# A hybrid encoder layer: the first modulation moved from VectorE to TensorE, filter loads to GpSimd's queue, the last gate computed late

## The chip, the cores and the metric

The kernel runs on one core of a Trainium2 chip. The metric is the device time of one execution in microseconds. Before the change three runs gave 1537.08, 1530.63 and 1531.85 us; the median is 1531.85 us.

The engines are called by their short names: PE is TensorE (matmuls; PEld its weight loads), DVE is VectorE, ACT is ScalarE, POOL is GpSimd and SP is SyncE. SP, ACT and POOL can issue DMAs; a name with q behind it (SPq) is an engine's instruction queue. Every engine executes its instructions in a fixed order.

## The reference

One layer over 1024 positions of width 1024, in float32. A conditioning vector c gives six vectors of 1024 (shift, scale and gate for two sub-layers). The first sub-layer normalises x, scales and shifts it, projects it, runs four mixers on groups of the projection and adds the gated output. The second is a SwiGLU with its own shift, scale and gate.

```python
mod = silu(c) @ mod_w + mod_b              # 6 x 1024
s1, b1, g1, s2, b2, g2 = split(mod, 6)     # shift, scale, gate, twice
u = (rms_norm(x) * (1 + b1) + s1) @ w_in
y = concat(ssd(u), neighbourhood_attention(u), mlstm(u), hyena(u))
x = x + g1 * (y @ w_out)
h = rms_norm(x) * (1 + b2) + s2
x = x + g2 * ((silu(h @ w_gate) * (h @ w_up)) @ w_down)
out = rms_norm(x) * final_g
```

The Hyena mixer convolves with long filters. They come from a small network of sines over the positions (`hyena_mlp`), a last matrix `w3`, a decay in time, a norm over the positions, and a discrete Fourier transform in which 16-point parts are done by additions on DVE and the rest by matmuls with tables. There are two filter orders.

## The kernel before, in words

Precise matmuls are made of three float32r products: a value is split into a high part and a remainder (`split`), and hi\*hi, lo\*hi and hi\*lo are added up in one PSUM bank. The normalised, modulated and transposed input stands in 16 tiles, `hhi[k]` and `hlo[k]` for k = 0 to 7, each 128 x 1024. Projections are groups of 256 columns (`w_group` loads and splits the weights; `gemm_t` makes, for each of two 128-column parts j, two 512-position halves h of 24 matmuls each, L493).

`build` states the order in which work is written down, and a planner of the framework puts each engine's instructions in a fixed order by readiness and that order. So instructions of several stages stand mixed in an engine's queue. The start of the program is written down so:

- `hyena_mlp` (L693 on): two layers of the sine network, each a matmul and seven DVE operations (`sin_layer`, L682 to L687) and one on ACT.
- `start` (L398 on): the first modulation. Its weights, 8 MB, are loaded by SP as 16 tiles of 512 KB into the slots that `hhi` and `hlo` take later (L416). Quarter q holds the shift and scale columns of k = 2q and 2q + 1. For three of the quarters DVE adds up eight weighted tiles into an accumulator of 128 x 512 (L420, L422); for quarter 3 ACT makes the products (L425) and POOL adds them (L427). The sum over partitions comes from transposes on PE and a reduction on DVE (L447, L449).
- Between the second and the third of these rounds the first part of `hyena_filters` (L720 on) is written: for eight blocks of positions a matmul with `w3` (L736), the decay loaded by SP into one of two buffers (L739), and DVE and ACT operations (L741 to L750); the norm is summed on PE (L746).
- Then the eight tiles of x are loaded (L435), squared on ACT (L437), scaled by DVE (L442), and for two halves h and eight k transposed on PE (L460), modulated on ACT (L462) and split (L235 on DVE; the remainder, L239, on POOL for even k and on DVE for odd k).
- The rest of `hyena_filters`: for each order and two sums q the Fourier transform; its nine matmul steps (L763, L765) each need a table that SP loads into one of three buffers (L761).

The second modulation is spread out. `modulation2` (L1485 on) adds up eight 512-column accumulators on DVE from 64 loads of 256 KB (L1494; two load buffers, two accumulators; L1496, L1498), which are stored to DRAM, while the Hyena convolutions and the SSD projections run; `modulation2_sums` (L1504 on) loads them again before the mLSTM and sums over partitions, for the gates g1 and g2 with a matmul by ones, and stores the gates to DRAM (`K.gd`). `attention` loads g1, and `ffn` loads g2 right after its second loop.

`ffn` has two loops over 22 blocks of hidden columns (matmuls at L1603) and a last stage, the down projection (L1742). Its buffers are numbered slots of 4 KB per partition; a tuple of slots is taken in turn. `psr` takes slots 27, 0, 1, 2 in turn, so the last block's `psr` is in slot 0. The last stage's weights are loaded to `wdr` and split to `wdh` and `wdl`:

```python
raw = S.tile([P, 2, H], F32, (17, 9, 10, 11), "wdr")
wh = S.tile([P, 2, H], F32R, (18, 12, 13, 14), "wdh")
wl = S.tile([P, 2, H], F32R, (21, 15, 16, 8), "wdl")
```

## Time and profile before

| | us |
|---|---|
| median of three runs | 1531.85 |
| the profiled execution | 1531.33 |
| its span, first to last instruction | 1529.5 |
| PE busy | 1412.3 (92%) |
| DVE busy | 1043.3 (68%) |
| ACT busy | 527.6 (34%) |
| POOL busy | 91.4 (6%) |

The shares are averages over stages with different limits. Matmuls are pipelined: one that is given as 0.39 us can start 0.23 us behind the one before it, so the distance of two starts, not the length, is what a matmul costs. A float32 matmul (not float32r) appears as two records. A wait is put down to what ended last before the waiting instruction began.

### The profile page before, as it was taken

The numbers are of one execution on the slowest core, as the hardware profiler recorded it, in microseconds if no ns is written. First come the engines' busy times: TensorE is split into PE (matmuls) and PEld (weight loads), VectorE is DVE, ScalarE is ACT, GpSimd is POOL, SyncE is SP. The second block draws the span as 40 slices with busy tenths as digits, with TensorE's granted clock in tenths as the row PEclk, the third lists the DMA queues.
The fourth block names the chain that finished last, engine by engine and source line by source line (L and its number), as shares of the span: only waits on it lengthen the run. The fifth ranks groups of instructions, "written<-read, shape, count | busy, mean of one in ns | idle before, by whom it ended". The sixth has DMA issues, their size and how long they took to land.

```text
span 1529.5 us, 19231 instructions
## 1 busy us (share of the span) xinstructions
PE 1412.3 (92%) x6849; PEld 1141.0 (75%) x6849; DVE 1043.3 (68%) x2004; ACT 527.6 (34%) x958; POOL 91.4 (6%) x143
## 2 busy tenths in 40 slices
PE   2589979998998998989989999999999999999997
PEld 0366768876797777867767777888888888888886
DVE  7998977977847684687865476477777766335327
ACT  2522221232242342333456775322222223224222
POOL 2110000000102231230000000000000000000000
PEclk9789999999998999999999999999999999999999
DMA  6534467577653325476426457554444448643402
GB/s 247 194 104 143 128 197 230 185 225 226 190 185 110 105 87 155 125 265 203 154 87 217 150 170 276 201 180 164 148 144 153 149 164 305 222 149 123 153 1 110
DMA packets 134899, 257.02 MB, mean 168 GB/s; under 512 B 24703, under 2 KB 69663, under 8 KB 134804
## 3 DMA queue, kind: packets, MB, share of 16 engines
q1 hardware_dynamic: 111508, 228.50, 45.4%
q10 hardware_dynamic: 22688, 25.99, 4.8%
q0 software_dynamic: 608, 1.31, 0.3%
q8 instruction: 54, 0.88, 0.2%
q14 instruction: 41, 0.34, 0.1%
HBM read 195.17 MB, written 60.59 MB: 167 GB/s over the span
## 4 chain that ended last, share of the span: by engine, by line
PE 74%; DVE 13%; DMA 5%; issue 2%; ACT 2%; POOL 2%; SPq 0%; DVEq 0%; ACTq 0%; POOLq 0%
PE dps L1742 14%; PE X L1603 12%; PE gps L493 9%; PE Z L1603 8%; PE Y L1603 8%; PE gps L505 4%; PE gps L1554 3%; PE nS L1427 2%; PE ops L1554 1%; DMA mxw<-modw 1%; PE nS L1405 1%; DVE wlo L239 1%; PE kps L763 1%; PE mpa L1339 1%; DVE acc L422 1%
## 5 line engine op out<-in xcount | busy, mean ns | idle before, releaser
L1742 PE MATMUL dps<-wdh,ah 128*128 128x512 f32 x352 | 136.9, 389 | 0.0
L1742 PE MATMUL dps<-wdh,al 128*128 128x512 f32 x352 | 136.9, 389 | 0.0
L1742 PE MATMUL dps<-wdl,ah 128*128 128x512 f32 x352 | 136.9, 389 | 0.0
L493 PE MATMUL gps<-hhi,whi 128*128 128x512 f32 x320 | 130.7, 408 | 3.8 <-ACT nt L529 3.8
L493 PE MATMUL gps<-hlo,whi 128*128 128x512 f32 x320 | 129.6, 405 | 0.0
L493 PE MATMUL gps<-hhi,wlo 128*128 128x512 f32 x320 | 129.0, 403 | 0.0
L1603 PE MATMUL Z<-hp,wgh 128*128 128x512 f32 x352 | 95.4, 402 | 1.9 <-ACT ps L1658 1.6
L239 DVE TENSOR_TENSOR al<-ar,ah 128x1024 fp32r<-128x1024 f32 x44 | 53.4, 1222 | 47.9 <-ACT ah L233 47.9
L505 PE MATMUL gps<-whi,hhi 128*128 128x256 f32 (+1 forms) x256 | 77.5, 303 | 1.5 <-ACT z L529 1.5
L1603 PEld LDWEIGHTS Z<-hp,wgh 128*128 128x128 f32 x352 | 63.7, 188 | 19.8 <-ACT ps L1658 5.3
L505 PE MATMUL gps<-whi,hlo 128*128 128x256 f32 (+1 forms) x256 | 77.2, 302 | 0.0
L505 PE MATMUL gps<-wlo,hhi 128*128 128x256 f32 (+1 forms) x256 | 77.1, 301 | 0.0
L1742 PEld LDWEIGHTS dps<-wdl,ah 128*128 128x128 f32 x352 | 66.1, 188 | 13.8
L1742 PEld LDWEIGHTS dps<-wdh,al 128*128 128x128 f32 x352 | 66.1, 188 | 13.7
L1742 PEld LDWEIGHTS dps<-wdh,ah 128*128 128x128 f32 x352 | 66.1, 188 | 13.6
L493 PEld LDWEIGHTS gps<-hhi,whi 128*128 128x128 f32 x320 | 60.6, 189 | 19.5 <-ACT nt L529 5.0
L493 PEld LDWEIGHTS gps<-hhi,wlo 128*128 128x128 f32 x320 | 60.5, 189 | 13.8 <-issue 1.6
L233 ACT CAST ah<-ar 128x1024 fp32r<-128x1024 f32 x44 | 45.7, 1048 | 72.5 <-PE dps L1742 42.7
L493 PEld LDWEIGHTS gps<-hlo,whi 128*128 128x128 f32 x320 | 60.6, 189 | 12.4 <-issue 0.8
L1603 PE MATMUL X<-A,t4s 128*128 128x512 f32 x264 | 63.4, 389 | 0.0
L239 DVE TENSOR_TENSOR wdl<-wdr,wdh 128x1024 fp32r<-128x1024 f32 x22 | 26.9, 1224 | 53.1 <-ACT wdh L233 53.1
L1498 DVE SCALAR_TENSOR_TENSOR mxacc<-mxw,cond,mxacc 128x512 f32<-128x512 f32 x56 | 42.0, 750 | 29.2 <-DMA mxw<-modw 28.9
(500 smaller groups left out, 3240.5 us busy)
## 6 DMA issues: line engine op xcount, KB each, us to landing
wg<-wg SPq DMA_DIRECT2D x44, 512.0 KB
ar<-ad SPq DMA_DIRECT2D x44, 512.0 KB
mxw<-modw SPq DMA_DIRECT2D x64, 256.0 KB
raw<-w_in SPq DMA_DIRECT2D x28, 512.0 KB
psd<-ps SPq DMA_DIRECT2D x22, 512.0 KB
psr<-psd SPq DMA_DIRECT2D x22, 512.0 KB
wu<-wu SPq DMA_DIRECT2D x22, 512.0 KB
wdr<-wd SPq DMA_DIRECT2D x22, 512.0 KB
```

The lines of the kernel that those rows point to most:

```text
L233: nc.scalar.copy(hi, src)
L239: e.tensor_tensor(lo, src, hi.bitcast(F32), op=ALU.subtract)
L422: V.scalar_tensor_tensor(acc, in0=w, scalar=c, in1=acc, op0=ALU.mult, op1=ALU.add)
L493: nc.tensor.matmul(ps, lhsT=w[:, k, c], rhs=x[k][:, t], start=n == 0, stop=n == len(seq) - 1)
L505: nc.tensor.matmul(ps, lhsT=x[k][:, t], rhs=w[:, k, :N], start=n == 0, stop=n == len(seq) - 1)
L763: nc.tensor.matmul(ps, lhsT=tab[:, la], rhs=y[:, 0], start=True, stop=not cx)
L1339: nc.tensor.matmul(pa[:, 2 * j + dr], lhsT=sds[dr][:, h], rhs=va[:, h], start=True, stop=True)
L1427: nc.tensor.matmul(pb[:, 448:512], lhsT=pT[:w * 40, n], rhs=vw[:w * 40, n, c:c + 64], start=n == 0, stop=n == len(chunks) - 1)
L1498: V.scalar_tensor_tensor(acc, in0=mt, scalar=K.cond[:, k:k + 1], in1=acc, op0=ALU.mult, op1=ALU.add)
L1554: K.nc.tensor.matmul(ps, lhsT=l, rhs=r, start=n == 0, stop=n == 5)
L1603: nc.tensor.matmul(ps, lhsT=w[a][:, k], rhs=x[k][b], start=start and n == 0, stop=n == 11, skip_group_check=not start)
L1742: nc.tensor.matmul(acc[i], lhsT=x[:, ts], rhs=m, start=f == 0 and n == 0, stop=f == NF - 1 and n == 2)
```

## The change

1. The first modulation is done by matmuls. For each quarter q eight fp32 matmuls multiply a column of silu(c) (128 x 1) by 512 columns of weights and add up in one row of PSUM. DVE copies the row to SBUF, four matmuls of one row by one column turn it into columns, and DVE adds the bias. ACT and POOL have no part in it. `start` becomes a generator that `build` advances in steps.
2. The order written down: `hyena_mlp`, loads and squares of x tiles 0 to 3, weights of quarter 0, the first projection's weights, the first part of the filters, weights of quarters 1 to 3, x tiles 4 to 7, then for each quarter its modulation and its two k of the first half; then the first half of the first projection (both j), the second half of the input, and the second half of the projection. The four PSUM banks of the first projection are handed to `hyena`.
3. The filters' loads (w3, decay, skip, tables; 58 in all) are issued by POOL and no longer by SP.
4. `modulation2` makes six accumulators, with one accumulator buffer and three load buffers. The gate g2 is computed in `ffn`, written down at the fifth block of its second loop, from eight loads of 512 KB with 128 x 1024 operations, and stays in slot 17. `wdr`, `wdh` and `wdl` move by a slot: their first tiles are now in 18, 21 and 0.

```diff
     with ExitStack() as e4:
         hf = hyena_filters(K, fl)
-        start(K, hp, Tags(pool("st", e4), tm=2), lambda: next(hf), lambda: w0.extend(w_group(K, G_HY + 2, first=False)))
+        st = start(K, hp, Tags(pool("st", e4)))
+        hyena_mlp(K, fl)
+        next(st)
+        next(st)
+        w0 = w_group(K, G_HY + 2, first=False)
+        next(hf)
+        next(st)
+        pss = [[gemm_half(K, *w0, j, 0)] for j in range(2)]
+        for _ in st:
+            pass
+        for j in range(2):
+            pss[j].append(gemm_half(K, *w0, j, 1))
     for _ in hf:
         pass
-mp = Tags(rpool("m2", right), mxw=2)
+mp = Tags(rpool("m2", right), mxw=3)
...
+    def modulation(q):
+        ps = K.pm.tile([P, 512], F32, tag="m", name="mps")[0:1]
+        for k in range(NK):
+            nc.tensor.matmul(ps, lhsT=K.cond[:, k:k + 1], rhs=mts[4 * q + k // 2][:, k % 2], start=k == 0, stop=k == NK - 1)
+        row = mts[4 * q + 3][0:1, 1]
+        V.tensor_copy(row, ps)
+        mc = K.pm.tile([P, 512], F32, tag="m", name="mcs")[:, :4]
+        for i in range(4):
+            nc.tensor.matmul(mc[:, i:i + 1], lhsT=row[:, i * P:(i + 1) * P], rhs=K.ones[0:1, 0:1], start=True, stop=True)
...
+    norm(0)
+    K.hhi, K.hlo = [], []
+    for q in range(4):
+        modulation(q)
+        for k in (2 * q, 2 * q + 1):
+            columns(0, k)
+    yield
+    for n in range(4, 8):
+        square(n)
+    norm(1)
+    for k in range(NK):
+        columns(1, k)
...
-            nc.sync.dma_start(dc[:, 0], d["c_decay"][:, j])
+            nc.gpsimd.dma_start(dc[:, 0], d["c_decay"][:, j])
...
-                nc.sync.dma_start(tab, d["c_tf"][k][:, 0:3:2] if q == 0 else d["c_tf"][k][:, 0:2])
+                nc.gpsimd.dma_start(tab, d["c_tf"][k][:, 0:3:2] if q == 0 else d["c_tf"][k][:, 0:2])
...
-    for n in range(8):
-        acc = sp.tile([P, 512], F32, "mxacc", bufs=2)
+    for n in range(6):
+        acc = sp.tile([P, 512], F32, "mxacc")
...
+def weighted_rows(K, S, c0, acc, slots):
+    nc, d = K.nc, K.d
+    for k in range(NK):
+        mt = S.tile([P, D], F32, slots, "mwt")
+        nc.sync.dma_start(mt, d["modw2"][k * P:(k + 1) * P, c0:c0 + D])
+        if k == 0:
+            nc.vector.tensor_scalar_mul(acc, mt, K.cond[:, 0:1])
+        else:
+            nc.vector.scalar_tensor_tensor(acc, in0=mt, scalar=K.cond[:, k:k + 1], in1=acc, op0=ALU.mult, op1=ALU.add)
+
+def modulation_g2(K, S, slots):
+    nc, d = K.nc, K.d
+    acc = S.tile([P, D], F32, slots[0], "g2")
+    weighted_rows(K, S, 3 * D, acc, slots[1:])
+    bb = S.tile([P, D], F32, slots[1:], "g2b")
+    nc.sync.dma_start(bb, d["modbg"][1:2].broadcast_to([P, D]))
+    for h in range(2):
+        hs = slice(h * 512, (h + 1) * 512)
+        ps = K.pg.tile([P, 512], F32, tag="g", name="mgp")
+        nc.tensor.matmul(ps, lhsT=K.ones, rhs=acc[:, hs], start=True, stop=True)
+        nc.vector.tensor_tensor(acc[:, hs], bb[:, hs], ps, op=ALU.add)
+    return acc
...
     for f in range(NF):
+        if f == 4:
+            g2 = modulation_g2(K, S, (17, 18, 21))
...
-    g2 = S.tile([P, D], F32, 0, "g2")
-    nc.sync.dma_start(g2, K.gd[1])
...
-            raw = S.tile([P, 2, H], F32, (17, 9, 10, 11), "wdr")
+            raw = S.tile([P, 2, H], F32, (18, 9, 10, 11), "wdr")
...
-            wh = S.tile([P, 2, H], F32R, (18, 12, 13, 14), "wdh")
-            wl = S.tile([P, 2, H], F32R, (21, 15, 16, 8), "wdl")
+            wh = S.tile([P, 2, H], F32R, (21, 12, 13, 14), "wdh")
+            wl = S.tile([P, 2, H], F32R, (0, 15, 16, 8), "wdl")
```

## Rows read from the trace of the kernel before

**Rows 1.** The page, busy time: engine, us (share of the span), instructions.

```profile
PE 1412.3 (92%) x6849; PEld 1141.0 (75%) x6849; DVE 1043.3 (68%) x2004; ACT 527.6 (34%) x958; POOL 91.4 (6%) x143
```

**Rows 2.** Busy time by stage: from:to us, length, engines, granted clock, DMA share, GB/s.

```profile
0.00:40.00 40.00, 10.60 (x21) 2.98 (x22) 31.46 (x44) 10.96 (x17) 10.82 (x13) 1.00 0.69 248
40.00:86.00 46.00, 26.28 (x107) 17.29 (x108) 43.70 (x94) 25.45 (x42) 7.78 (x6) 0.70 0.55 180
86.00:120.00 34.00, 30.97 (x131) 25.15 (x129) 32.25 (x63) 7.85 (x12) 4.14 (x3) 0.95 0.33 101
120.00:206.00 86.00, 78.07 (x345) 58.38 (x343) 79.81 (x164) 24.67 (x39) 0.30 (x1) 0.98 0.42 132
206.00:430.00 224.00, 207.00 (x982) 172.68 (x983) 172.39 (x320) 55.03 (x100) 6.13 (x11) 0.98 0.68 216
980.00:1280.00 300.00, 300.00 (x1325) 248.26 (x1324) 214.78 (x296) 77.54 (x92) 0.00 (x0) 1.00 0.49 166
```

**Rows 3.** The same of line L493 alone: PE, PEld, granted clock, DMA.

```profile
86.00:120.00 34.00, 24.30 (x96) 18.07 (x96) 0.95 0.33 101
```

**Rows 4.** Groups of VectorE up to 95 us: busy us, mean ns, idle before.

```profile
L422 DVE SCALAR_TENSOR_TENSOR acc<-mw,cond,acc 128x512 f32<-128x512 f32 x21 | 18.6, 885 | 0.4
...
L686 DVE SCALAR_TENSOR_TENSOR su<-sn,su 128x512 f32<-128x512 f32 x6 | 6.3, 1042 | 0.1
...
L741 DVE TENSOR_TENSOR hf<-fps,dc 128x512 f32<-128x512 f32 x8 | 5.5, 687 | 1.5 <-DMA dc<-c_decay 1.0 <-PE fps L736 0.4
...
L449 DVE TENSOR_REDUCE mc<-psm 128x4 f32<-128x512 f32 x4 | 2.6, 686 | 0.0
```

**Rows 5.** Timeline near 11 us: start us, length us, engine line operation.

```profile
11.25 1.63 POOL L427 TENSOR_TENSOR acc<-acc,pr 128x512 f32<-128x512 f32 x1 [10.31 <-ACT pr L425]
11.68 1.75 DVE L686 SCALAR_TENSOR_TENSOR su<-sn,su 128x512 f32<-128x512 f32 x1
```

**Rows 6.** Busy time of the first two stretches of 10 us, as in rows 2.

```profile
0.00:10.00 10.00, 1.97 (x4) 0.32 (x4) 2.48 (x5) 1.65 (x3) 0.41 (x5) 1.00 0.59 188
10.00:20.00 10.00, 1.97 (x4) 0.29 (x4) 9.73 (x10) 4.48 (x8) 5.94 (x5) 1.00 1.02 412
```

**Rows 7.** Timeline of TensorE: fp32 matmuls of 256 columns, and transposes.

```profile
63.25 6.53 PE L460 MATMUL tps<-ident,x 128*128 128x128 f32 x34 [8.20 <-DVE x L442]
...
99.49 1.06 PE L763 MATMUL kps<-yk,tab 128*128 128x256 f32 x2
100.34 0.83 PE L765 MATMUL kps<-yk,tab 128*128 128x256 f32 x2
...
110.31 0.59 PE L765 MATMUL kps<-yk,tab 128*128 128x256 f32 x2
110.74 0.59 PE L763 MATMUL kps<-yk,tab 128*128 128x256 f32 x2
```

**Rows 8.** A DMA issued by POOL in the timeline; landing times of line L1172.

```profile
405.34 0.53 POOL L1172 DMA_DIRECT2D mlm<-c_mlm  x1
...
DMA to landing us min/median/max: 4.0/4.3/4.6
```

**Rows 9.** The page's costliest groups, as in rows 4.

```profile
L239 DVE TENSOR_TENSOR wdl<-wdr,wdh 128x1024 fp32r<-128x1024 f32 x22 | 26.9, 1224 | 53.1 <-ACT wdh L233 53.1
L1498 DVE SCALAR_TENSOR_TENSOR mxacc<-mxw,cond,mxacc 128x512 f32<-128x512 f32 x56 | 42.0, 750 | 29.2 <-DMA mxw<-modw 28.9
```

**Rows 10.** Waits: who waited for whom, us in total, times, longest us.

```profile
DVE uv L1701 <- PE Y L1603: 43.8, 22, 2.3
...
SPq L761 <- PE kps L765: 60.4, 23, 9.5
```

**Rows 11.** Timeline at the end of the second loop.

```profile
1279.90 0.39 PE L1742 MATMUL dps<-wdh,ah 128*128 128x512 f32 x1
...
1280.35 0.39 PE L1742 MATMUL dps<-wdl,ah 128*128 128x512 f32 x1
...
1283.72 0.69 DVE L1707 TENSOR_TENSOR a<-uv,psr 128x512 f32<-128x512 f32 x1
```

More of the change, by code (lines that the diff above doesn't have):

```diff
@@ L332, in build @@
         K.acr = dp.tile([64, P], F32, name="acr")
-        K.macc = [dp.tile([P, 512], F32, name=f"macc{n}") for n in range(8)]
-        K.gd = dp.tile([2, P, D], F32, name="gd")
+        K.macc = [dp.tile([P, 512], F32, name=f"macc{n}") for n in range(6)]
+        K.gd = dp.tile([P, D], F32, name="gd")
         K.xd = [dp.tile([P, D], F32, name=f"xd{n}") for n in range(8)]
@@ L395, in build, with start @@
             _dump(K, dump)
[L398 removed]
+def start(K, hp, sp):
     nc, d = K.nc, K.d
     V = nc.vector
[L403 to L427 removed]
@@ new lines, in square, with load_w @@
+    def square(n):
+        jk = K.so.tile([P, D], F32, "st", name="jk")
+        nc.scalar.activation(jk, xs[n], AF.Square, accum_out=ss[:, n:n + 1])
+    for n in range(4):
+        load_x(n, sp.tile([P, D], F32, f"x{n}"))
+        square(n)
+    yield
+    mts = []
+    def load_w(q):
+        for k in range(0, NK, 2):
+            t = hp.tile([P, 2, 512], F32, name="mw", tag=f"{('hhi', 'hlo')[k // 2 % 2]}{2 * q + k // 4}")
+            nc.sync.dma_start(t, d["modw1"][q, :, k:k + 2].rearrange("p k s c -> p k (s c)"))
+            mts.append(t)
@@ new lines, in start @@
+    load_w(0)
+    yield
+    for q in (1, 2, 3):
+        load_w(q)
+    xt = [K.wp.tile([P, NK, 288], F32, t, name="x").rearrange("p a b -> p (a b)") for t in ("whi", "wlo")]
+    for n in range(4):
+        load_x(4 + n, xt[n // 2][:, n % 2 * D:(n % 2 + 1) * D])
+    norm(0)
[4 more added lines that the diff above has]
+            columns(0, k)
+    yield
+    for n in range(4, 8):
+        square(n)
+    norm(1)
+    for k in range(NK):
+        columns(1, k)
@@ L480, in w_group, with gemm_half @@
     return whi, wlo
[L483 to L495 removed]
+def gemm_half(K, whi, wlo, j, h):
+    c = slice(j * P, (j + 1) * P)
+    t = slice(h * 512, (h + 1) * 512)
+    ps = K.pg.tile([P, 512], F32, tag="g", name="gps")
+    seq = [(w, x, k) for k in range(NK) for w, x in ((whi, K.hhi), (whi, K.hlo), (wlo, K.hhi))]
+    for n, (w, x, k) in enumerate(seq):
+        K.nc.tensor.matmul(ps, lhsT=w[:, k, c], rhs=x[k][:, t], start=n == 0, stop=n == len(seq) - 1)
+    return ps
+def gemm_t(K, whi, wlo, j):
+    return [gemm_half(K, whi, wlo, j, h) for h in range(2)]
 def gemm_n(K, whi, wlo, i, N=256):
@@ L1507, in modulation2_sums @@
     mv = K.mod2
-    for n in (0, 1, 6, 7, 2, 3, 4, 5):
-        acc = sp.tile([P, 512], F32, "mxacc", bufs=2)
+    for n in range(6):
+        acc = sp.tile([P, 512], F32, "mxacc")
         nc.sync.dma_start(acc, K.macc[n])
-        if 2 <= n < 6:
+        if n >= 2:
             ps = K.pm.tile([P, 512], F32, tag="m", name="m2p")
```

107 lines of the change are left out of this document (27 added, 80 removed).

## Prediction

> **What bounds the kernel now.** I read the page's busy shares first: TensorE (PE) is busy 1412.3 of the 1529.5 us [rows 1], so a gain can only come from the 117 us in which it idles or from a stretch where something else sets the pace. The table by stage says where those lie [rows 2]. Up to 86 us TensorE works 10.6 + 26.3 = 36.9 us and VectorE (DVE) 31.5 + 43.7 = 75.2 us: the start is VectorE's. From 86 to 206 us both are nearly full (PE 109.0, DVE 112.1 of 120 us). From 206 to 430 us PE idles 17 us and DVE 52 us: neither is full, the wait of one for the other counts. From 980 to 1280 us PE is busy 300.0 of 300 us and DVE has 85 us free: there only a delay can happen. The landmark for the start is the first projection group, 96 matmuls of L493, all between 86 and 120 us [rows 3].
>
> **The start, by VectorE.** The change takes from it 21 weighted adds of L422 (18.6 us) and 4 reductions of L449 (2.6), 21.2 us [rows 4] (three short products that start the sums go too and are not counted). It also takes POOL's 7 adds away. While one of them ran (11.25 us, 1.63 long), a DVE operation of L686 took 1.75 us [rows 5]; six of L686 cost 6.3 us, and at the 0.687 of another 128x512 operation (L741) they would cost 4.1 [rows 4], so 2.2 us come back there. I count 1.7 more for the other operations of that layer that stood beside POOL, an estimate from the same lengthening: 3.9. It adds 4 row copies of 512 elements from PSUM; no such row exists, a 128x512 read of PSUM costs 0.69 (L741), so 4 x 0.69 = 2.8. Sum: -21.2 - 3.9 + 2.8 = -22.3 us. Up to 120 us DVE worked 107.4 and idled 12.6 [rows 2]; now it needs 85.1, and I leave it 13 us of idling, because the sine layers of the filters no longer have the weighted adds between their steps and wait as much as before. The state of 120 us is then reached at about 98.
>
> **The start, by TensorE.** 32 fp32 matmuls of one column by 512 are added. The nearest rows are the 256-column fp32 pairs of L763 and L765: 0.85 us apart after a wait (99.49 to 100.34), 0.43 apart when TensorE has run for a while (110.31 to 110.74) [rows 7]; for 512 columns I take twice that, 0.86 or 1.70. At 0.86 they cost 27.5 us, at 1.70 54.4. The first of them needs the small tables, four tiles of x and one of weights, 3.1 MB: 188 GB/s up to 10 us and 412 GB/s behind it [rows 6] put that at 10 + (3.1 - 1.9)/0.412 = 13 us. All that is loaded up to the last modulation tile, 13.3 MB, is there by 38 us, ahead of TensorE. From 13 us on: 27.5 for the modulation; 8 x 0.86 + 8 x 0.43 = 10.3 for the filters' first part, which is queued ahead of it; 32 transposes at 6.53/34 = 0.19 [rows 7], 6.1; 1 for the small column matmuls: 57.9 us, where the first projection could start at the latest (86 now). Then 48 matmuls at 0.226 (two steps of the products of the last stage, 1279.90 to 1280.35, are 0.45) [rows 11], 10.8; the second half's transposes, 6.1; 48 more, 10.8; and the 131 - 96 = 35 records, 17 fp32 matmuls, that now stand between them [rows 2, 3], 7.5: 93 us. VectorE's 98 is the later, so I take 120 - 98 = 22 us of gain. The 16 transposes of the accumulators and the ACT work on the last quarter also go; neither engine is full there, so I count them at nothing. Ends for this part: nothing, if the matmuls go at 1.70 (93 + 27 = 120), and 30, if VectorE idles no more than half as long as assumed.
>
> **Loads from POOL's queue.** 58 issues move from SP (16 of the decay, 36 tables, 4 of w3, 2 of skip). POOL takes 0.53 us for one, and the landing takes 4.0 to 4.6 us for 512 KB [rows 8]. How much longer that is than on SP no row here tells: nothing at least, the whole landing at most; I use 2 us. Behind a waiting issue on POOL stand the next table loads and the even-numbered hlo subtractions, for which the projection waits. SP in turn loses 60.4 us of waits of L761, in 23 pieces of up to 9.5 [rows 10], that stood ahead of raw weight loads. From one gain and one loss I take a loss of 2 us (ends: 5 gained, 8 lost, two round trips of 4 us in the second order's first part).
>
> **Modulation 2 in the middle.** 16 of 64 weighted adds leave this stage: 16 x 0.75 = 12 us of DVE. DVE waits 28.9 us for their loads [rows 9], and a third buffer lets each load start one addition sooner. But with one accumulator in place of two, each of five groups must wait for the store of the one before it, at most about 4 us each (the landing of [rows 8] is the nearest row). TensorE's 17 idle us of this stage [rows 2] are the most that can be won; DVE's relief meets matmuls that fill up anyway. I take 5 gained; ends 15 gained, and 5 lost if four of five stores are seen in part.
>
> **g2 in the feed-forward.** Eight operations of 128x1024 (twice 0.69, 1.4 us) and two additions of 0.69 are 12.5 us on DVE, put in at the fifth of 22 steps. DVE waits there for TensorE 43.8 us in 22 places, 2.0 each [rows 10]; one such operation fits into each wait. Cost 1 us, ends 0 and 5 (nine loads that each hold VectorE 0.52 us, as 28.9 us over 56 additions do now [rows 9], with the next step's weights late by as much). At the end of that loop the first wdl tile moves to a slot that the last step's psr still holds. psr is read last by L1707 at 1283.72 + 0.69 = 1284.4; plus 1.2 for the subtraction [rows 9] is 1285.6. The first product with wdl ran at 1280.35 [rows 11]: 5.3 us apart. 14 further products can go ahead without wdl, 14 x 0.226 = 3.2. Cost 2 us, ends 0 and 7 (the full wait, and a slower clock behind it).
>
> **The sum.** -22 + 2 - 5 + 1 + 2 = -22 us. The profiled execution took 1531.33 us (1529.5 of span and 1.8 around it); the median of the three runs is 0.5 above it, 1531.85. 1531.3 - 22 = 1509.
>
> **A rule of the skill against POOL's queue.** The row first: DVE and POOL held each other up at 11.68 us [rows 5], while POOL issued its DMA at 405.34 in 0.53 us [rows 8] among additions on DVE. The Trainium skill, page "SBUF — State Buffer", section "Who interferes with whom", says that copies, casts and tensor_scalar operations of VectorE can take the port pair that it shares with GpSimd for their whole length, and section "SBUF: two separate sides" that GpSimd cannot write the descriptors of its loads meanwhile. No row here has a cast beside such an issue. It is rival 2.
>
> **The rivals.**
> 1. TensorE stays at its lower clock through the modulation. For it: the granted clock is 0.70 from 40 to 86 us, where TensorE is busy a little over half the time [rows 2]. Against: the 32 matmuls follow one another. At 0.70 the 27.5 us become 39, 93 becomes 105, the gain 15 and, with the columns pushed into VectorE's full stretch, about 12: 1519. Wholly at 1.70 us each: 1531.
> 2. Casts hold POOL's issues. About 14 issues fall into the stretch with the 16 casts; each waits for one, by length at most the 0.7 of a 128x512 operation: 14 x 0.7 = 10 us later, 1519. It was told above which page has this.
> 3. The start gains 30 and the middle stage its 15, with nothing lost behind: 1531.3 - 45 + 3 = 1490 or a little over. For it: PE's sum ends before DVE's, and the waits for mxw are long [rows 9]. Against: DVE and PE are both nearly full from 120 to 206 us.
> 4. Slower: POOL works in order, and its eight hlo subtractions stand behind table loads that wait for a free buffer, thus for TensorE's kps matmuls, which wait for the table before. Now that wait is 60.4/23 = 2.6 us on SP [rows 10]; with a landing 2 us later it is 4.6, and 8 x 4.6 = 37 us: 1509 + 37 = 1546. It decides from 22/8 = 2.8 us for each subtraction. Against: the subtractions are early, and only three tables are wanted by then.
> 5. The change doesn't do what it says: the modulation matmuls are placed behind work that waits for VectorE, and the first projection starts no earlier than 80 us. What is left is VectorE's relief, used up by waiting: 1529.
>
> **How the numbers follow.** Forecast 0.50, rival 1 0.14, rival 2 0.05, rival 3 0.13, rival 4 0.13, rival 5 0.05. Half a per cent, 7.7 us, is about what a measurement of this kernel can tell from no change. Faster (below 1524): the forecast, most of rivals 1 and 2, rival 3, 0.75 after a little for their slow ends. Within: rival 5 and those ends, 0.11. Slower (above 1539): rival 4 and a little of the unknown in the feed-forward, 0.14. The range goes from rival 3, 1490, to 1534, which takes in the full low clock; outside are rival 4 and a little below 1490. The forecast's own range is 1500 to 1518.
>
> **What would show it.** First L493 matmul at 58 to 70 us and the 96th at about 98 in place of 120; the modulation matmuls 0.86 us apart at a granted clock near 1; no L422 on DVE; the stage that begins at 206 us some 20 us earlier; mxw waits of DVE well under 28.9 us; a PE wait of some 2 us before the first product with wdl. Wrong, if hlo on POOL follows a table load by over 2.8 us again and again, if the modulation matmuls stand 1.7 apart, or if the gain of the start is gone by 206 us.

## The result: slower by 1.6 per cent, and the profile after

The changed kernel takes 1555.8 us (median of 4 runs), the kernel before 1531.2 beside it: ratio 1.0155, 95% interval [1.0128, 1.0181]. The forecast was 1509, with a range up to 1534. The profiled run took 1557.7, its span 1555.9, 26.4 us more than that of before (1529.5). The page's busy line, which answers to [rows 1]: TensorE has 47.6 us more, VectorE 19.7 less.

```profile
PE 1459.9 (94%) x6929; PEld 1156.9 (74%) x6929; DVE 1023.6 (66%) x1972; ACT 524.7 (34%) x952; POOL 111.4 (7%) x194
```

The table by stage, as in [rows 2]:

```profile
0.00:40.00 40.00, 17.25 (x44) 6.70 (x44) 20.44 (x41) 15.47 (x23) 7.73 (x18) 0.91 0.92 354
40.00:86.00 46.00, 43.42 (x131) 13.48 (x130) 32.57 (x65) 9.63 (x15) 7.29 (x10) 0.93 0.22 82
86.00:120.00 34.00, 31.41 (x141) 24.37 (x142) 28.71 (x50) 16.74 (x25) 9.58 (x9) 0.95 0.21 62
120.00:206.00 86.00, 78.91 (x343) 58.91 (x342) 77.48 (x166) 22.16 (x36) 20.16 (x34) 1.00 0.44 138
206.00:430.00 224.00, 204.04 (x985) 171.15 (x984) 172.87 (x323) 56.91 (x102) 7.58 (x14) 0.98 0.63 202
980.00:1280.00 300.00, 299.46 (x1315) 246.00 (x1314) 216.10 (x296) 77.42 (x94) 0.00 (x0) 1.00 0.51 173
```

Up to 86 us VectorE worked 20.4 + 32.6 = 53.0 us, 22.2 less than before. That is the relief of the forecast (22.3), and yet at 86 us next to nothing is won: VectorE idled for all of it. The first projection starts at 83.8 us (86.0 before; 58 to 70 in the forecast), and its 96th matmul at 118.9 (119.5; about 98). What has fallen behind are the kps matmuls of the filters' DFT: the first starts at 97.3 us in place of 81.8, at 120 us 17 of their 128 records have begun in place of 40, and the last starts at 223.3 in place of 211.5.

To see where the 26.4 us arose I took, in each profile, the starts of a few operations that end a stage: the first fps of the hyena stage (L790 before, L810 after), the last yps of its end ("z"), the first mS and the last mpi of the mLSTM, the first Z and the last X of the two feed-forward loops, the last dps. Each number is a difference of two such starts, in us; in brackets the granted clock of the mLSTM stage.

| kernel | to first fps | to z | to mS | mLSTM (clock) | to Z | to last X | to last dps | ratio to before |
|---|---|---|---|---|---|---|---|---|
| before | 218.4 | 224.1 | 180.8 | 50.6 (1.00) | 139.2 | 466.6 | 239.3 | |
| before_again | 218.6 | 225.4 | 178.3 | 50.6 (1.00) | 137.7 | 465.9 | 239.4 | 1.0011 [0.9993, 1.0029] |
| changed | 230.2 | 212.3 | 177.4 | 66.7 (0.75) | 145.6 | 468.8 | 244.3 | 1.0155 [1.0128, 1.0181] |
| after_again | 232.0 | 215.3 | 178.9 | 65.4 (0.77) | 145.6 | 470.2 | 245.6 | 1.0156 [1.0121, 1.0191] |
| old_start | 220.7 | 214.8 | 177.2 | 54.2 (0.97) | 144.6 | 471.0 | 242.7 | 1.0088 [1.0061, 1.0116] |
| new_start | 232.7 | 224.6 | 179.4 | 58.7 (0.84) | 138.6 | 467.8 | 239.3 | 1.0123 [1.0076, 1.0170] |
| wdl_slot | 230.7 | 214.1 | 179.0 | 52.9 (1.00) | 147.0 | 468.9 | 239.4 | 1.0131 [1.0085, 1.0178] |
| mod_first | 228.7 | 215.2 | 178.0 | 52.9 (1.00) | 146.9 | 469.9 | 242.8 | 1.0140 [1.0099, 1.0181] |
| kps_early | 225.7 | 214.9 | 177.9 | 61.1 (0.84) | 145.6 | 470.6 | 245.6 | 1.0162 [1.0129, 1.0194] |
| mod_kps | 234.3 | 214.7 | 177.9 | 61.3 (0.84) | 145.6 | 471.6 | 244.3 | 1.0177 [1.0126, 1.0227] |
| half_mod | 218.9 | 214.8 | 179.8 | 61.3 (0.84) | 146.8 | 469.6 | 242.7 | 1.0124 [1.0083, 1.0166] |
| dc_sp | 225.2 | 216.4 | 176.5 | 65.5 (0.77) | 145.6 | 469.5 | 244.2 | 1.0153 [1.0115, 1.0190] |
| old_mx2_wdl | 218.2 | 217.1 | 182.1 | 59.0 (0.81) | 140.0 | 468.7 | 239.3 | 1.0029 [1.0008, 1.0050] |
| g2_late | 219.5 | 215.6 | 180.3 | 56.0 (0.94) | 149.9 | 470.7 | 242.7 | 1.0141 [1.0111, 1.0171] |
| mid_only | 219.0 | 220.5 | 198.6 | 56.8 (0.82) | 137.3 | 465.7 | 239.4 | 1.0122 [1.0084, 1.0159] |
| md_again | 232.8 | 214.0 | 178.0 | 63.7 (0.95) | 139.4 | 471.6 | 244.3 | 1.0148 [1.0116, 1.0180] |
| best_again | 218.6 | 218.2 | 181.5 | 59.3 (0.91) | 136.2 | 469.8 | 239.4 | 1.0036 [1.0012, 1.0059] |

The first profiles of both kernels give the account of the 26.4 us: start +11.8, hyena stage -11.8, up to the mLSTM -3.4, mLSTM +16.1, from there to the first Z +6.4, second loop with what leads to it +2.2, last stage +5.0: 26.3. A row of the table is one execution. The two kernels' second profiles differ from their first by up to 3.0 us outside the mLSTM, and the -3.4 on the way to the mLSTM is +0.6 there (178.3 and 178.9). The start's +11.8 is +13.4 there.

### The profile page after: what moved, and what is told of

It reads as the page before. It is cut to its first block, busy times and chain, and to the rows that moved or that the text cites. A ratio compares the mean times of both kernels' runs of the same rounds, so it can differ in the third digit from the quotient of the medians.

```text
span 1555.9 us, 19338 instructions
## 1 busy us (share of the span) xinstructions
PE 1459.9 (94%) x6929; PEld 1156.9 (74%) x6929; DVE 1023.6 (66%) x1972; ACT 524.7 (34%) x952; POOL 111.4 (7%) x194
## 4 chain that ended last, share of the span: by engine, by line
PE 76%; DVE 12%; DMA 5%; issue 3%; ACT 2%; POOL 1%; SPq 0%; DVEq 0%; ACTq 0%; POOLq 0%
PE dps L1788 14%; PE X L1649 11%; PE gps L509 9%; PE Z L1649 8%; PE Y L1649 7%; PE gps L1600 4%; PE gps L525 4%; PE nS L1447 2%; PE nS L1425 1%; PE mps L439 1%; PE ops L1600 1%; PE mpa L1359 1%; DMA dc<-c_decay 1%; DVE wlo L239 1%; DMA mxw<-modw 1%
## 5 line engine op out<-in xcount | busy, mean ns | idle before, releaser
L1788 PE MATMUL dps<-wdh,ah 128*128 128x512 f32 x352 | 137.3, 390 | 0.0
L525 PE MATMUL gps<-whi,hhi 128*128 128x256 f32 (+1 forms) x256 | 76.8, 300 | 1.5 <-ACT z L549 1.5
L1649 PEld LDWEIGHTS Z<-hp,wgh 128*128 128x128 f32 x352 | 63.7, 188 | 18.8 <-ACT ps L1704 4.2
L525 PE MATMUL gps<-wlo,hhi 128*128 128x256 f32 (+1 forms) x256 | 76.1, 297 | 0.0
L509 PEld LDWEIGHTS gps<-hhi,whi 128*128 128x128 f32 x320 | 60.6, 189 | 20.7 <-ACT nt L549 6.2
L525 PE MATMUL gps<-whi,hlo 128*128 128x256 f32 (+1 forms) x256 | 76.0, 297 | 0.0
L1649 PEld LDWEIGHTS X<-A,t4s 128*128 128x128 f32 x264 | 49.5, 188 | 10.5 <-issue 0.3
```

The lines of the kernel that those rows point to most:

```text
L509: K.nc.tensor.matmul(ps, lhsT=w[:, k, c], rhs=x[k][:, t], start=n == 0, stop=n == len(seq) - 1)
L525: nc.tensor.matmul(ps, lhsT=x[k][:, t], rhs=w[:, k, :N], start=n == 0, stop=n == len(seq) - 1)
L1649: nc.tensor.matmul(ps, lhsT=w[a][:, k], rhs=x[k][b], start=start and n == 0, stop=n == 11, skip_group_check=not start)
L1788: nc.tensor.matmul(acc[i], lhsT=x[:, ts], rhs=m, start=f == 0 and n == 0, stop=f == NF - 1 and n == 2)
```

## Experiments

**Which half costs what.** Two kernels take one half each: old_start has the start of the kernel before and all else as changed, new_start the reverse.

```diff
 # old_start, against the changed kernel
-st = start(K, hp, Tags(pool("st", e4)))
...
+start(K, hp, Tags(pool("st", e4), tm=2), lambda: next(hf), lambda: w0.extend(...))
 # new_start, against the kernel before: the reverse, with gemm_half and the loads from POOL
```

> The changed kernel with the start of the kernel before (VectorE's weighted adds, filters' loads from SP), everything else as changed: third load buffer and one accumulator in modulation 2, g2 in the second loop, its slots. Theory A (the losses and gains have places of their own: start +12 at 206 us, middle -12 by 430 us, a low clock in the mLSTM stage +16, second loop +3, last stage +5): the hyena stage ends some 12 us earlier than in the kernel before (z at 430 in place of 442), the wait of 6.5 us before the first product with wdl is there again; the total is 1531 - 12 + 3 + 5 = 1527 if the clock stays up in the mLSTM stage, 1543 if it falls there again. Rival B (the middle won nothing of its own, the stage only absorbs a late start): z at 442, total 1539, or 1555 with the low clock.

> The kernel before with the new start alone (modulation on TensorE, filters' first part ahead of it, filters' loads from POOL, halves of the first projections apart); modulation 2 in eight parts with two buffers and two accumulators, g2 early, old slots. Theory A: +12 at 206 us and nothing that takes it back, z at 454 in place of 442, total 1543, or 1559 with a low clock in the mLSTM stage. Rival B (the middle absorbs the late start): z at 442, total 1531, or 1547 with the low clock. Either way no wait of 6.5 us before the first product with wdl.

Rival B falls. The hyena stage takes 214.8 us with the changed middle under the old start, 212.3 and 215.3 under the new one, and 224.6 with the old middle, so the middle won 9 to 12 us of its own. The new start costs 14.3 in new_start. Both totals end above theory A's lower cases: old_start has +5.4 from the mLSTM to Z that I had not listed, and new_start an mLSTM of 58.7 us.

**The slot of wdl.**

```diff
-ps1 = S.tile([P, 2, H], F32, (27, 0, 1, 2), "psr")
+ps1 = S.tile([P, 2, H], F32, (0, 27, 1, 2), "psr")
```

> The changed kernel with one edit: psr takes its four slots in the order 0, 27, 1, 2, so that the last step of the second loop holds slot 27 and the first wdl finds slot 0 free one step earlier. If the slot is the cause of the 6.5 us wait and of the slower pace of TensorE behind it: no such wait, the products at 0.23 us each from the first on, total 1556 - 5 to 7 = 1550. Rival (the wait is for the loading of wd or for VectorE's queue at the end of the loop): a wait of over 4 us stays, total 1554 to 1556. The rest of the kernel, the low clock at 650 to 700 us too, is expected as it was, since nothing ahead of the second loop is touched.

The 6.5 us named there are about the sum of two waits, that of the product (3.0) and that of its weight load (3.4), which are the same 3 us. The changed kernel's TensorE at the end of the second loop, which answers to [rows 11]: 16 products with wdh go ahead, then it waits, and the next 8 run at 2.99/8 = 0.37 us in place of 0.23 (granted clock 0.67 from 1308 to 1311 us).

```profile
1301.20 0.39 PE L1788 MATMUL dps<-wdh,ah 128*128 128x512 f32 x1
...
1304.62 0.39 PE L1788 MATMUL dps<-wdh,al 128*128 128x512 f32 x1
1308.04 2.99 PE L1788 MATMUL dps<-wdl,ah 128*128 128x512 f32 x8 [3.02 <-DVE wdl L239]
```

The same place in wdl_slot: the third product is one with wdl, nobody waits.

```profile
1292.85 0.39 PE L1788 MATMUL dps<-wdh,ah 128*128 128x512 f32 x1
1293.07 0.39 PE L1788 MATMUL dps<-wdh,al 128*128 128x512 f32 x1
1293.30 0.39 PE L1788 MATMUL dps<-wdl,ah 128*128 128x512 f32 x1
```

The slot was the cause: 239.4 us for the last stage, as before; 242.7 to 245.6 in all kernels with the old slot order and the late g2. That part of the loss is 3.4 to 6.3 us. What I did not expect is the mLSTM of 52.9 us, with nothing changed ahead of it.

**The order at the start.** In the changed kernel the modulation matmuls stand behind the filters' first part, and TensorE works in order (timeline of TensorE; idle before in brackets):

```profile
28.37 1.60 PE L756 MATMUL fps<-w,h 64*128 64x512 f32 x4 [3.07 <-ACT h L708]
31.81 1.19 PE L766 MATMUL nps<-s,ones 128*128 128x256 f32 x2 [1.85 <-POOL hf L768]
...
42.74 2.07 PE L756 MATMUL fps<-w,h 64*128 64x512 f32 x2 [1.50 <-DVE hf L761]
44.74 1.22 PE L766 MATMUL nps<-s,ones 128*128 128x256 f32 x2
45.90 1.86 PE L439 MATMUL mps<-mw,cond 128*1 128x512 f32 x2
```

Three edits of the order alone: mod_first puts the filters' first part behind the modulation, kps_early puts the filters' DFT (its kps matmuls) ahead of the first projections, mod_kps does both.

```diff
-next(hf)                     # filters' first part
 next(st)                     # modulation, first columns
+next(hf)                     # mod_first, mod_kps
+next(hf)                     # kps_early, mod_kps: the first order's DFT
 pss = [[gemm_half(K, *w0, j, 0)] for j in range(2)]
```

> The changed kernel with the filters' first part issued behind the modulation in place of ahead of it. Order theory (the modulation matmuls stood behind fps and nps matmuls that wait for VectorE and for the decay loads): modulation matmuls from 14 to 24 us on, 0.86 us each where the clock is up, the first projection matmul at 55 to 68 us in place of 86, and the stage that starts at 206 us at least 10 us earlier than in the changed kernel; total 1536 to 1546 if that is kept to the end, with the low clock in the mLSTM stage as it was. Rival (VectorE's sum of work binds the start, or the filters' loads from POOL do): the first projection is early, but VectorE now has the filters' part behind it; at 206 us nothing is won, total 1552 to 1558.

> The changed kernel with the rest of the filters' first order (its DFT, the kps matmuls and table loads) issued ahead of the first projections in place of behind both halves; nothing else. Theory C (VectorE starves from 56 to 97 us because the kps matmuls that free its yk buffers stand behind the modulation and 48 projection matmuls on TensorE): the first kps at 75 to 85 us in place of 97, VectorE's busy time from 60 to 100 us over 34 in place of 26.6, and the last kps and the first fps of the hyena stage at least 8 us earlier than in the changed kernel (223, 230). Total 1540 to 1548, the rest as it was. Rival (the start is bound by the sum of what waits for each other, as it was when the modulation went first and the state at 206 us did not move): kps earlier, but the first fps of the hyena stage still at 228 to 232, total 1549 to 1557.

> The changed kernel with the modulation first, then both parts of the filters' first order (the DFT with its kps matmuls too) ahead of the first projections; mod_first and kps_early together. If the two waits that these removed one by one (3 and 4.5 us at the first fps of the hyena stage) add up: that first fps at 220 to 223 in place of 230. If one wait only takes the place of another: 225 to 230 still. If their removal opens the start as the forecast had it: 200 to 214.

mod_first does at the start what it should: modulation from 18.5 us, first projection at 56.9 (the forecast had 57.9). At the first fps 1.5 us of this are left (3.3 by the second profile of the changed kernel): there its rival is right, though the total, 1550.3, lies between the two ranges. kps_early brings the first kps from 97.3 to 85.8 and the last from 223.3 to 207.6, but the first fps only 4.5 us forward, half of what theory C wanted; its first fps lies between theory and rival. Both together are worse than either: 234.3, beyond all three ranges expected. So one wait takes the place of another, and more.

**TensorE's share.** half_mod leaves out every second modulation matmul.

```diff
-for k in range(NK):
+for k in range(0, NK, 2):
     nc.tensor.matmul(ps, lhsT=K.cond[:, k:k + 1], rhs=mts[4 * q + k // 2][:, k % 2], ...)
```

> The changed kernel with every second of the 32 modulation matmuls left out (the sums lack half of their terms; all loads stay). Theory E (the start pays for the 27.5 us that the modulation adds to TensorE, which has no room for them up to 206 us once its matmuls stand in front): TensorE's mps busy time falls from 30 to 15 us, the first projection matmul comes at 70 to 76 us in place of 83.8, and the first fps of the hyena stage at 216 to 222 in place of 230. Rival F (the order sets the start: VectorE waits for kps behind the projections whatever the modulation costs): the first projection 8 to 14 us earlier, but the first fps of the hyena stage at 226 or later.

The modulation matmuls of the changed kernel, all and then the copies of its rows (duration min/median/max in ns, first and last start):

```profile
L439 PE MATMUL mps<-mw,cond x64: 590/592/1057, 45.9 to 83.2; 128*1 128x512 f32 x64
L441 DVE COPY mw<-mps x4: 672/679/679, 56.9 to 83.9; 1x512 f32<-1x512 f32 x4
```

Those of half_mod:

```profile
L439 PE MATMUL mps<-mw,cond x32: 590/592/1057, 47.9 to 72.2; 128*1 128x512 f32 x32
```

16 matmuls at 0.86 us are 13.8 us of TensorE. The first projection comes at 72.8 (83.8), the first fps at 218.9: 11.3 us earlier than in the changed kernel, 13.1 earlier than in its second profile. So TensorE's time goes through to the first fps at 0.8 to 0.95 us for each us, where the order alone gave 1.5 and 4.5. Theory E holds. The granted clock is a rival: it was 1.00 up to 120 us in half_mod, 0.91 to 0.95 in the first profile of the changed kernel. But the second profile had 1.00 up to 86 us, and its first fps came at 232.0, no earlier. By it (an estimate) the whole 27.5 us cost 23 to 26, and the new start without them would reach the first fps at 204 to 208, 10 to 14 us ahead of the kernel before.

**POOL's queue.** dc_sp puts the filters' loads back on SP.

```diff
-nc.gpsimd.dma_start(dc[:, 0], d["c_decay"][:, j])     # and w3, skip, tab
+nc.sync.dma_start(dc[:, 0], d["c_decay"][:, j])
```

> The changed kernel with the filters' loads (decay, tables, w3, skip) back on SP's queue. Forecast's term for that queue: 2 us lost on POOL. If POOL's queue costs: VectorE's waits for the decay loads, 6 us together in the changed kernel, fall under 3, the first modulation matmul comes 2 to 5 us before 45.9, and the first fps of the hyena stage 2 to 6 us before 230. If SP is worse (its raw weight loads then stand behind table loads that wait): first fps at 231 to 240.

The longest waits of VectorE up to 120 us in the changed kernel (us, times, longest), without those of the sine layer:

```profile
DVE hf L761 <- DMA dc<-c_decay: 6.2, 5, 1.8
DVE mw L441 <- PE mps L439: 4.1, 3, 2.8
DVE hhi L235 <- ACT tm L463: 3.6, 5, 1.3
DVE ln0v L248 <- ACT jk L420: 3.5, 1, 3.5
DVE mod L446 <- PE mcs L444: 3.3, 3, 1.4
```

The first of them in dc_sp:

```profile
DVE hf L761 <- DMA dc<-c_decay: 0.6, 2, 0.3
```

The first fps comes 5.0 us earlier, by the end of the expected 2 to 6 (6.8 against the second profile). A decay load up to 60 us lands 5.0 us after its issue by POOL and 3.7 after its issue by SP (medians). POOL's queue cost 5 to 7, not 2. In the total nothing of it is seen (1.0153): the hyena stage is 4.1 us longer (216.4), so that z comes at 441.6 us, 442.5 in the changed kernel.

**The middle, and the order behind the mLSTM.** old_mx2_wdl is old_start with two load buffers and the slot order of wdl_slot; mid_only is the kernel before with three buffers and one accumulator; g2_late is the kernel before with the late g2 and its slots.

```diff
-mp = Tags(rpool("m2", right), mxw=2)                # before
+mp = Tags(rpool("m2", right), mxw=3)                # mid_only
-acc = sp.tile([P, 512], F32, "mxacc", bufs=2)
+acc = sp.tile([P, 512], F32, "mxacc")               # mid_only
```

> The kernel with the start of before and the changed rest, but two buffers for modulation 2's loads in place of three, and psr's slots in the order 0, 27, 1, 2. Its order of instructions from the first output projection to the second loop is nearly that of the kernel before (12 of PE's rows differ, 148 with three buffers). Theory D (the 6 to 8 us lost between the end of the mLSTM and the first Z come from the order of instructions there, nothing else): that stretch 138 to 141 us, as in the kernel before (139.2) and in new_start (138.6, the same order to the row), against 144.6 to 147.0 in the four others. Rival (it is lost to something that the change does there, such as the late reading of the gate): 144 to 147 again. The last stage without the wait for wdl. In the middle: if the third buffer made the gain, z is at 440 to 443; if the 16 additions less made it, at 434 to 437. Total 1528 to 1536 by theory D, 1534 to 1542 by the rival.

> The kernel before with three buffers and one accumulator in modulation 2; all eight parts and g2 as before. If the third buffer made the middle's gain of 7 us: z at 433 to 437 in place of 442. If the 16 additions less made it: z at 440 to 445. The stretch from the end of the mLSTM to the first Z has another order of instructions (112 of PE's rows differ): by theory D it is not 139.2 but anything from 138 to 147. No wait for wdl; second loop as before. Total 1524 to 1538.

> The kernel before with modulation 2 in six parts and g2 in the second loop with its slots, two buffers and two accumulators as before. If the 16 additions less made the middle's gain: z at 434 to 438; if the third buffer did: 440 to 444. Second loop +2 to +4 us (466.6 before from the first Z to the last X), the wait for wdl 3 to 6.5 us and the last stage 242 to 244 us in place of 239.3. From the end of the mLSTM to the first Z the order of instructions is another (176 of PE's rows differ). Theory D: 144 to 147 there. Total 1532 to 1544.

The 16 additions less make most of the gain: with two buffers the hyena stage takes 217.1 and 215.6 us (224.1 and 225.4 before); the third buffer, with one accumulator, wins 3.6 to 4.9 (220.5), and mid_only's z, 439.5, lies between its two ranges. VectorE's wait for mxw falls from 28.9 us [rows 9] to 8.3 in the changed kernel:

```profile
DVE mxacc L1518 <- DMA mxw<-modw: 8.3, 9, 2.9
```

That wait does not measure the gain: it is 10.9 us in mid_only, which won less, and 21.6 and 19.0 with two buffers in old_mx2_wdl and g2_late, which won more.

mid_only's total, 1548.2, lies 10 us above its range, for a reason of its own: one accumulator makes the eight sums ahead of the mLSTM a chain. From the first of them (matmuls mgp) to the last transpose m2p it takes 588.2 to 622.7 us in mid_only, 585.9 to 606.2 before, 14.2 us longer; up to the mLSTM it needs 18 to 20 us more. The transposes in mid_only, and those in the kernel before:

```profile
L1514 PE MATMUL m2p<-ident,mxacc x16: 270/273/302, 608.9 to 622.7; 128*128 128x128 f32 x16
```

```profile
L1514 PE MATMUL m2p<-ident,mxacc x16: 270/273/415, 596.7 to 606.2; 128*128 128x128 f32 x16
```

Theory D holds where it was put to the test. From the first mS on new_start has the order of the kernel before to the row, and needs 138.6 us from the mLSTM to Z. The changed kernel's order on PE differs from it in 148 rows between the first output product and Z by the count of the expectation above, and it needs 145.6 us there; old_mx2_wdl, with 12 rows, 140.0. In the traces, from the last mpi to Z, the changed kernel's order on PE stands to the row in nine profiles: its own two, old_start, wdl_slot, mod_first, kps_early, mod_kps, half_mod and dc_sp. They need 144.6 to 147.0 us, five of them 145.6. Where the order is that of the kernel before but for 6 of some 630 rows at most (new_start, old_mx2_wdl, mid_only, best_again), it is 136.2 to 140.0. The code of that stage is the same in all. The stage in the kernel before and in the changed one (columns as in [rows 2]):

```profile
673.90:813.10 139.20, 129.40 (x636) 98.80 (x634) 103.61 (x256) 63.11 (x128) 5.20 (x5) 0.95 0.48 161
```

```profile
686.60:832.20 145.60, 133.13 (x635) 101.02 (x634) 104.30 (x254) 63.38 (x127) 3.64 (x3) 0.93 0.46 152
```

TensorE idles 2.7 us more (12.5 and 9.8) and is busy 3.7 us longer at the lower granted clock. What differs at the stage's start, in the kernel before (start, length):

```profile
670.05 1.28 DVE L1542 SCALAR_TENSOR_TENSOR wor<-wor,pc,g 128x1024 f32<-128x1024 f32 x1
...
674.08 1.11 PE L1339 MATMUL mpa<-mkv,msd 128*128 128x65 f32 x8
674.99 1.18 PE L1554 MATMUL gps<-wowh,yh 128*128 128x512 f32 x4
```

and in the changed kernel:

```profile
686.96 1.97 PE L1359 MATMUL mpa<-mkv,msd 128*128 128x65 f32 x8
...
689.31 1.28 DVE L1588 SCALAR_TENSOR_TENSOR wor<-wor,pc,g 128x1024 f32<-128x1024 f32 x1
...
691.71 2.07 PE L1600 MATMUL gps<-wowh,yh 128*128 128x512 f32 x4 [2.79 <-ACT wowh L233]
```

Before, VectorE scales the first output weights ahead of the mLSTM's last operations, now behind them, and TensorE waits 2.8 us. That is part of the 6.4; the rest I did not trace row by row. md_again has a third order there and needs 139.4: another order need not be a worse one. g2_late's total lies 6 us above its range; its order behind the mLSTM is the slowest (149.9).

**The clock in the mLSTM.** after_again and before_again are the two kernels without an edit.

> The changed kernel once more, without an edit: which of its stage times come again. Theory: all that follows from the order comes again to about 1 us (first fps at 230, z at 442 to 444, 145 to 147 from the end of the mLSTM to the first Z at equal clock, second loop 468 to 471, last stage 242 to 246). The mLSTM itself (66.7 us at a granted clock of 0.75, 52 to 53 at 1.0 in three others) doesn't: 53 to 67. Rival: the low clock there follows from the changed kernel's order: 0.7 to 0.8 and 64 to 68 us again. Total 1550 to 1558.

> The kernel before once more, without an edit, for a second profile. If the low clock in the mLSTM belongs to the changed kernels: granted clock 0.95 to 1.0 from the first mS to the last mpi, 50 to 52 us, as in its first profile. If any order can have it and the first profile was lucky: under 0.9 and over 55 us. All other stages again to about 1 us: first fps of the hyena stage 218, z 442, 139 us to the first Z behind the mLSTM, second loop 466.6, last stage 239.3.

The way from the mLSTM to Z comes again in the changed kernel (145.6) and to 1.5 us in the kernel before (137.7), and so does the mLSTM's clock in each: 0.77 and 1.00. The first fps (232.0) and z (447.3) of after_again miss their ranges, by 1 to 3 us. Its mLSTM, 65.4 us at 0.77, lies in the wide range of the theory and in the narrow one of the rival, that the low clock follows from the changed kernel's order; other profiles with that order are against the rival. The mLSTM stage of the kernel before, of the changed kernel, and of mod_first, whose order there is that of the changed kernel (columns as in [rows 2]):

```profile
623.30:673.90 50.60, 50.26 (x338) 41.36 (x334) 40.71 (x121) 18.46 (x34) 12.70 (x20) 1.00 0.59 201
```

```profile
619.90:686.60 66.70, 65.89 (x344) 53.96 (x341) 40.84 (x121) 17.99 (x34) 13.41 (x21) 0.75 0.48 155
```

```profile
621.90:674.80 52.90, 51.80 (x344) 42.67 (x341) 40.37 (x121) 17.29 (x33) 13.67 (x21) 1.00 0.52 169
```

Same matmuls, same order, 13.8 us apart by the clock alone. The nine profiles named above have one order of TensorE here too, and clocks from 0.75 to 1.00. And new_start, whose order here is that of the kernel before, has 0.84:

```profile
636.70:695.40 58.70, 58.42 (x335) 48.08 (x334) 42.31 (x122) 18.97 (x35) 14.40 (x21) 0.84 0.52 178
```

So the order in this stage does not decide it. A rival that no run separates is the chip: of the nine, three profiles from one chip have 0.97 to 1.00 and five from two others 0.77 to 0.84 (the changed kernel's first has no chip on record), but new_start's 0.84 is from the first of these. The four runs of wdl_slot lie between 1544.4 and 1556.0 us, and its profile is of the fastest: a kernel's time spreads by nearly as much as this clock is worth.

To test whether it falls for want of large matmuls I added some: ml_extra, best_extra and before_extra have two behind each mD group, with a PSUM tile of their own; md_again and best_again repeat the first matmul of the group in its own tile.

```diff
+pd = K.pg.tile([P, 512], F32, tag="g", name="extra")                    # the *_extra kernels
+for n in range(2):
+    nc.tensor.matmul(pd, lhsT=sel1[:, dr], rhs=mbd..., start=n == 0, stop=n == 1)
...
-nc.tensor.matmul(ps, lhsT=gr[:, cs], rhs=oneh[:, dr], start=True, stop=False)
+for n in range(3):                                     # md_again; 2 in best_again
+    nc.tensor.matmul(ps, lhsT=gr[:, cs], rhs=oneh[:, dr], start=True, stop=n < 2)
```

> The changed kernel with 24 more matmuls of 512 columns in chunks 2 to 7 of the mLSTM (two behind each mD, of tiles that are there; their result is read by nobody). Theory G (TensorE's clock falls there because little but small matmuls is left once the projections between them run out): the granted clock from the first mS to the last mpi 0.95 to 1.0; the stage takes 52 + 24 x 0.23 = 58 us in place of 65 to 67, total 1546 to 1552. Rival (the clock falls for another reason, or from an earlier idling): 0.75 to 0.85 again, 70 us or more, total 1558 to 1564.

> The variant with the old start, two load buffers, one accumulator, g2 late and psr's other slot order (1532 where the kernel before had 1528), with the same 24 more matmuls. By theory G its mLSTM stage, 59.0 us at a granted clock of 0.81, takes 56 to 58 us at 0.95 or more, and the wo stage behind it keeps 140 if its order is kept, but the order behind the mLSTM is another now (270 of PE's rows differ from the kernel before), so 138 to 150. Total 1526 to 1542.

> The kernel before with the same 24 more matmuls. If its clock there is 1.0 anyway: 50.6 + 5.5 = 56 us for the mLSTM stage, and the total 1531 to 1545, the rest by another order behind the mLSTM. If the kernel before loses to the clock there in most of its runs and the profile didn't show it: total at or under 1528.

> The changed kernel with the first matmul of each mD group run three times (the sum starts anew each time, so the result is the same): 32 more matmuls of 512 columns in the mLSTM, 32 x 0.23 = 7.4 us of TensorE, no tile more. Theory G (the clock falls because little but small matmuls is left there): granted clock 0.95 to 1.0 from the first mS to the last mpi, 53 to 60 us in place of 65 to 67; total 1545 to 1554. Rival (it falls whatever stands there): 0.85 or less, 68 us or more, total 1558 to 1565. The stages ahead of it as in the changed kernel (first fps 230 to 232, z 442 to 447).

> The variant with the old start, two load buffers, one accumulator, g2 late and psr's other slot order, with the first matmul of each mD group run twice: 16 more, 3.7 us. Theory G: the mLSTM stage, 59.0 us at 0.81 without them, at 0.95 or more in 52 to 57 us; the stretch behind it 138 to 142 (its order is nearly that of the kernel before); total 1524 to 1531 beside 1528 to 1531 of the kernel before. Rival: 0.85 or less and 60 us or more, total 1533 to 1538.

The three extra kernels failed as experiments: 1.0652 [1.0630, 1.0673], 1.0617 [1.0574, 1.0659], 1.0557 [1.0530, 1.0585]. Their tile takes turns with those of the projections, which were thus held back behind the mLSTM: it takes 54 us at a clock of 0.96 to 0.97 in all three, but 217 to 220 us follow up to Z, and the stretch ahead of it, empty of them, has a clock of 0.67 to 0.68 (the last projection matmul of L525 starts at 753.3 us in ml_extra, at 652.3 in the changed kernel). md_again keeps the clock up as theory G says (0.95) and yet takes 63.7 us, over the 53 to 60 expected: what the clock gives back the added matmuls use up (32 x 0.23 = 7.4) and more. best_again has 0.91 in 59.3 us, between theory and rival; its total, 1535.4, is the rival's. All five kernels with added matmuls have 0.91 to 0.97, but some without them reach that too (old_start 0.97, mod_first 1.00): that large matmuls hold the clock up there fits this and is not shown. They don't pay. Neither old_mx2_wdl nor best_again beats the kernel before; no version here does.

## Why the prediction was wrong, step by step

1. **The start, VectorE's sum.** Right in its terms: work up to 120 us 81.7 (forecast 85.1, but for a state with more of the kps done), the row copies 0.68 each (0.69), the sine layers' operations 0.69 without POOL beside them (0.687).
2. **"I leave it 13 us of idling."** This is the step that failed: it idled 120 - 81.7 = 38.3. The waits above name 20.7 of it (3.6, 4.1 and 3.3 are the chain from the modulation's rows to hhi, of which the kernel before has 0.4; the decay loads take 6.2 in place of 1.0), the sine layers 9.8 more (7.5 before). Why is in the busy times: TensorE's added 27.5 us and VectorE's work alternate. Up to the first fps TensorE is busy 186.8 us in place of 156.7, VectorE 177.1 in place of 194.6, and VectorE's waits for TensorE are 29.3 in place of 14.4. I had made a sum for each engine (93 and 98) and taken the later, which holds only if neither waits for the other. The rows said it: from 86 to 206 us both were nearly full [rows 2], so TensorE had no room to give back what it was behind at 86. half_mod shows that TensorE's time decides, mod_first that the first projection's place does not.
3. **The start, by TensorE.** 0.86 us per matmul was right (0.43 for each of its two records). The place was not: 45.9 us for the first in place of 13, as rival 5 had it; its price (1529) was too low, since it counted no loss behind 80 us. Rival 1 is not the reason: the granted clock was 0.91 and 0.93 up to 86 us in the first profile and 1.00 in the second, with no smaller loss. Net start: -22 + 2 forecast, +11.8 measured, 31.8 of the 48.4 us by which the profiled run missed.
4. **POOL's queue.** 5 to 7 us in place of 2, within its ends. Rivals 2 and 4 were not seen: POOL issued a decay load in 0.55 us (0.53 in [rows 8]) and a table load in two pieces in 0.72 to 0.73 among VectorE's casts (98 to 108 us) as at 180 us. Its hlo subtractions waited for VectorE's hhi; the one at 98.93 us stood behind a table load that had waited 9.0 us for kps, but its hhi was itself ready only at 98.35, so that it lost 0.6 us where rival 4 needed 2.8 (groups of POOL up to 230 us, then the place):

```profile
L239 POOL TENSOR_TENSOR hlo<-tm,hhi 128x512 fp32r<-128x512 f32 x8 | 10.7, 1336 | 33.4 <-DVE hhi L235 25.5 <-issue 7.8
L759 POOL DMA_DIRECT2D dc<-c_decay x16 | 8.8, 548 | 46.5 <-DVE hf L761 42.1 <-DMA dc<-c_decay 4.2
...
97.92 0.43 DVE L235 CAST hhi<-tm 128x512 fp32r<-128x512 f32 x1 [1.29 <-ACT tm L463]
98.18 0.73 POOL L781 DMA_DIRECT2D tab<-c_tf  x1 [9.04 <-PE kps L783]
98.59 1.92 DVE L235 CAST hhi<-tm 128x512 fp32r<-128x512 f32 x1
98.93 1.28 POOL L239 TENSOR_TENSOR hlo<-tm,hhi 128x512 fp32r<-128x512 f32 x1
```

   What the Trainium skill, page "SBUF — State Buffer", section "Who interferes with whom", says of casts and the shared port pair shows no price in POOL's issues here. VectorE's casts beside POOL's subtractions did grow, to 1.92 and 1.49 us from 0.41; all 16 took 12.3 us, 11.2 before.
5. **The middle.** -9 to -12 in place of -5 in the hyena stage, mostly from the additions that left. The 3.4 more up to the mLSTM did not come again.
6. **g2 in the second loop.** Mean of the 13 profiles with the late g2 470.1 us against 466.5 of the four others (the extra kernels left out): 3.6 in place of 1, within the ends.
7. **The wdl slot.** 3.4 to 6.3 in place of 2, within 0 to 7, with 16 products ahead where I had 14; the slower clock behind it was named as part of the upper end.
8. **Not in the prediction at all:** the mLSTM (+16.1 in the first profile, 2.3 in wdl_slot and mod_first, where the clock stayed up) and the way from it to Z (+6.4), 22.5 of the 48.4 us. The second is shown to go with the order that the planner writes. Of the first it is shown that it is the clock; why it falls in one profile and not in another with the same order is open.

## What to carry to other kernels

Where two engines work by turns, moving work from the fuller to the other is a gain only as far as the other has room up to the end of that stretch: sum both, and put the waits that the mover now has on its own account. Where a planner writes the order, an edit changes stages whose code it does not touch; compare the orders before the times, and read each stage by its own landmarks. A slot taken over across the end of a loop cost its wait and the clock behind it here, and a rotation of the slots was all that it took.

## What the runs showed of the hardware

TensorE's granted clock fell from the upper level (2.4 GHz) to the lower (1.2 GHz) at about 650 us of the changed kernel without an idle moment in the records: it was busy for all of the 30 us from 620 to 650, and the matmuls around the fall follow each other (columns as in [rows 2], then the timeline).

```profile
620.00:640.00 20.00, 20.00 (x131) 16.84 (x132) 14.38 (x46) 7.55 (x14) 3.85 (x6) 1.00 0.27 70
640.00:650.00 10.00, 10.00 (x72) 8.52 (x71) 8.64 (x24) 2.11 (x4) 1.92 (x3) 1.00 0.23 65
...
660.00:680.00 20.00, 19.41 (x76) 15.61 (x74) 10.16 (x31) 3.51 (x7) 3.85 (x7) 0.50 0.81 287
```

```profile
648.89 0.71 PE L1335 MATMUL mS<-mqk 64*128 64x128 f32 x4
649.53 0.38 PE L525 MATMUL gps<-whi,hhi 128*128 128x256 f32 x1
649.84 0.86 PE L1335 MATMUL mS<-mqk 64*128 64x128 f32 x4
650.64 0.79 PE L1340 MATMUL mD<-oneh,mgr 128*128 128x512 f32 x1
```

It stayed at 0.50 from 660 to 700 us, though TensorE was busy 19.4 of the 20 us up to 680. The Trainium skill, page "TensorE: Matmul & The Clock Gate", section "Why this matters for your kernels", asks for no long idle gaps of TensorE between bursts of matmuls if the clock is to stay up. The wait for wdl above agrees (3.0 us of idling, then a granted clock of 0.67 up to 1311 us); here the measurement goes further: this stage lost the clock without idling.
